# Banded attention scores on the whole array: q's parts stacked by halves, k's parts doubled, and a table of put-off steps

## The chip, the cores and the metric

The kernel runs on one core of one Trainium2 chip. Its engines are TensorE (PE in the profile; PEld are its weight loads), VectorE (DVE), ScalarE (ACT), GpSimd (POOL) and SyncE (SP, which only issues DMAs). The metric is the device time of one execution in microseconds.

## What is computed

Two layers of an encoder over 512 tokens of 1024 channels, all in float32. Each layer projects x to the parts of two token mixers, projects their outputs, merges them by gates, adds and normalises, and then runs a feed-forward part with 4096 hidden channels. The part that matters is mixer A, attention within 128 tokens to either side:

```python
qa = _rope(qa.reshape(bsz, seq, 8, 64), cos, sin)      # 8 heads of 64
ka = _rope(ka.reshape(bsz, seq, 2, 64), cos, sin)      # 2 key heads, 4 queries' heads on each
oa, _ = _banded_attention(qa, ka, va, 128, a_sink)
...
# _banded_attention, for each block j of 128 queries
s = jnp.einsum('nqkgd,nskd->nkgqs', qj * scale, kj)    # kj: three blocks of keys
s = jnp.where(mask, s, -jnp.inf)
m = jnp.maximum(jnp.max(s, axis=-1), sink_b)
e = jnp.exp(s - m[..., None])
denom = jnp.sum(e, axis=-1) + jnp.exp(sink_b - m)
o = jnp.einsum('nkgqs,nskd->nqkgd', e, vj) / denom
```

Mixer B does the same over three groups of heads with dilated windows, without the sink.

## The kernel before

Precision comes from splitting: every operand of a product is kept as a high part in fp32r and a low part, the rest. `split` makes them (ACT copies into the high part, DVE subtracts), and a product is three matmuls: high by high, low by high, high by low (`mm3`, or `PASSES` for scores). Projections stream x (all 512 tokens) through 128x128 tiles of weights, 24 matmuls of 512 columns for an output tile of 128 channels. Weights come in fixed order through SP (`fetch`) and are split by `split`, or by `split_later`, which lets ACT write both parts and a DMA on POOL's queue add the source to the low one.

`attention_block` runs the mixers of a layer. Its start projects k, v and the first two q tiles of mixer A. A tile of q holds two heads, i on rows 0 to 63 and i+4 on rows 64 to 127, and k's tile holds the two key heads on the same halves of rows. `rope` rotates such a tile: DVE shuffles and multiplies, POOL multiplies, DVE adds (`t1`), and `split` gives the pair qh, ql. `pair_scores` (L435) then forms the scores of both heads from halves: a matmul of 64 rows for each head and pass, six of them for a step, of which the two heads' run as a pair.

What PE does when is written out by hand in this block. `unit_a(i)` is a generator of the work for q tile i: four score steps (blocks j, with 256, 384, 384, 256 keys; tiles sa), then transposes of the exponentials (pta) and their products with v (oa), then a scaling. `unit_b` and `mix_b` do that for mixer B. `filler` yields the projections one k-tile (three matmuls) at a time, in the order of `FLOW`: q tiles 2 and 3 of A, then q, k, v of B's groups (qb, kb, vb), gates g(0,t) and the output projections of A (y, tiles ya). The loop at the end of the block takes the first generator whose next step is ready by a forecast (`Forecast`, with assumed durations and `HOP` between engines), else one step of filler; a third count, `held["qk"] - held["free_qk"]`, limits how many q and k tiles are alive (5), and a filler that needs one stands still until a unit has ended its scores. The forecast decides only the order on PE. The other engines' order is set by a scheduler from the program; DVE and ACT serve the masks (`masked`, L432, DVE, reads a score bank), exponentials (L428, ACT) and splits in the order that comes out. There are two PSUM banks for scores, two for transposes, one for oa and three for projections. The name sa_1_2 stands for unit a1, block 2.

Of the kernel before, what the change touches and what calls it, by code (L numbers as in the profile page):

```python
# [10 lines left out]
F32 = mybir.dt.float32  # L11
F32R = mybir.dt.float32r
# [27 lines left out]
ACTIVE = 2  # L40

# [160 lines left out]
def build(nc, tc, plan, down, xT, xN, pT, wst, vec, rows, sink, cst, out):  # L202
# [3 lines left out]
    with ctx:  # L206
# [142 lines left out]
        def attention_block(l, av, rp, vt, OA, OB, begun):  # L349
# [21 lines left out]
            def rope(ps, dil, name):  # L371
# [6 lines left out]
                hi = av.tile([P, S], F32R, tag="qh", name="qh" + name, bufs=5)  # L378
                lo = av.tile([P, S], F32R, tag="ql", name="ql" + name, bufs=5)
# [60 lines left out]

            def weighted(o, vv, blk, r, pT, cols, first, last):
                both = vv[:, blk, r].rearrange("p h d -> p (h d)")
                nc.tensor.matmul(o, both, pT[0][:, cols], start=first, stop=False, skip_group_check=True)
                nc.tensor.matmul(o[:64], both[:, :64], pT[1][:, cols], start=False, stop=last, skip_group_check=True)
# [27 lines left out]
            def unit_a(i):  # L472
                q, k = held["qa", i], held["ka"]
# [245 lines left out]
            held = {"P": 0, "qk": 3, "free_qk": 0, "vv": 0}  # L719
# [6 lines left out]
            held["ka"] = rope(kps, False, f"ka{l}")  # L726
# [3 lines left out]
            held["qa", 0] = rope(q0, False, f"qa{l}_0")  # L730
            fc.take("mm")
            held["qa", 1] = rope(q1, False, f"qa{l}_1")
# [19 lines left out]
            def filler():  # L752
                def project(key, sigma_order):
# [3 lines left out]
                    held[key] = rope(ps, sigma_order, "_".join(str(v) for v in (l, *key)))  # L757

                for kind, *idx in FLOW:
                    if kind == "qa":  # L760
                        yield from project(("qa", *idx), False)
                    elif kind == "b":
# [5 lines left out]
                        side.append([v_unit(("vb", *idx), v, t, nm_), None])  # L768
# [20 lines left out]
            def slots(n, *keys):  # L789
                def ok():  # L790
                    if held["P"] + n > 4 or any(k not in held or fc.t < held[k][2] for k in keys):
# [5 lines left out]
            ga, waiting, live = [], {}, {}  # L797
# [10 lines left out]
            with tc.manual_schedule(engines={PE}):  # L808
                side.append([v_unit("va", va, t_va, f"va{l}"), None])
                fill, fill_ok, idle = filler(), None, 0  # L810
                while waiting or live or side or fill:
                    if waiting and len(live) < ACTIVE:
                        key = next(iter(waiting))
                        ok, make = waiting[key]
                        if ok():
                            del waiting[key]
                            live[key] = [make(), None]
                    moved = False
                    for key, g in [(None, g) for g in side] + list(live.items()):
                        if g[1] is None or g[1]():  # L820
                            try:
                                g[1] = next(g[0])
                            except StopIteration:
# [235 lines left out]
        for l in range(DEPTH):  # L1059
# [33 lines left out]
            for u in range(4):  # L1093
                gs = [gate(l, 1, t, vt, rp) for t in (2 * u, 2 * u + 1)]
# [271 lines left out]
```

## Time and profile before

| | us |
|---|---|
| runs | 1536.09, 1539.66, 1539.62 |
| median | 1539.62 |
| the profiled execution | 1536.4 |
| its span | 1534.6 |
| PE busy in it | 1512.5 (99%) |
| DVE, ACT, POOL busy | 1017.7, 763.7, 246.4 |
| attention stage, layer 0 and layer 1 | 245.70, 247.90 |

The profile is one execution, taken by the hardware profiler; its span is a little shorter than its time. PE's busy time is modelled, and matmuls overlap each other, so how long PE takes for something is read from the starts of matmuls. The attention stage here is the stretch from the transposes of va (29.2 us in layer 0) to the first gate of the second branch (274.9 us).

### The profile page before, as it was taken

The page shows a single profiled execution, that of the slowest core. Times are in us where ns is not written, and L with a number is a line of the kernel's source. Part 1 is how long each engine was busy: PE and PEld are TensorE (multiplying, and loading weights), DVE is VectorE, ACT ScalarE, POOL GpSimd, SP SyncE. Part 2 cuts the span into 40 slices and gives each one's busy share as a digit, 9 for nine tenths or more (in the row PEclk, how much of TensorE's full clock was granted, in tenths as well). Part 3 has the DMA queues.
Part 4 walks back from the last instruction along what each step waited for, and adds up shares of the span by engine and source line. Part 5 has one row for each costly group of instructions (what it writes and reads, how often), then busy time and mean ns, then how long its engine had stood idle before and what let it go on. Part 6 is the DMA issues. An engine that isn't in the chain of part 4 may idle for free.

```text
span 1534.6 us, 19685 instructions
## 1 busy us (share of the span) xinstructions
PE 1512.5 (99%) x7438; PEld 1243.0 (81%) x7438; DVE 1017.7 (66%) x1751; ACT 763.7 (50%) x1244; POOL 246.4 (16%) x213
## 2 busy tenths in 40 slices
PE   9999999999999999999999999999999999999996
PEld 7778888888888888888887888878888888888885
DVE  5666553558568777686876665534585776767868
ACT  5777764344344443444557776633442444444442
POOL 1212220110011120202012112111100201111022
PEclk9999999999999999999999999999999999999998
DMA  7544665345612414141355445574455233231403
GB/s 234 124 112 111 149 151 166 123 137 152 205 55 87 133 54 153 42 161 59 100 168 137 114 112 138 138 209 134 149 149 183 69 109 111 82 124 56 151 1 96
DMA packets 53951, 189.47 MB, mean 123 GB/s; under 512 B 6496, under 2 KB 6880, under 8 KB 53856
## 3 DMA queue, kind: packets, MB, share of 16 engines
q1 hardware_dynamic: 43200, 151.74, 30.0%
q0 software_dynamic: 9936, 36.18, 12.5%
q8 instruction: 58, 0.95, 0.3%
q10 hardware_dynamic: 720, 0.30, 0.1%
q14 instruction: 37, 0.30, 0.1%
HBM read 155.16 MB, written 4.19 MB: 104 GB/s over the span
## 4 chain that ended last, share of the span: by engine, by line
PE 88%; DVE 5%; DMA 3%; ACT 2%; issue 1%; POOL 0%; SPq 0%; POOLq 0%; DVEq 0%; ACTq 0%
PE dn L1018 16%; PE ps_up L281 8%; PE ps_up L280 8%; PE ps_up L282 8%; PE pg L288 2%; PE wo L288 2%; PE wo L287 2%; PE wo L286 2%; PE pg L286 2%; PE pg L287 2%; PE sa L439 1%; PE pta L417 1%; DMA raw<-wst 1%; PE sb L439 1%; PE ps_start L281 1%
## 5 line engine op out<-in xcount | busy, mean ns | idle before, releaser
L228 ACT CAST whi<-wst 128x1024 fp32r<-128x1024 f32 (+2 forms) x120 | 121.2, 1010 | 257.8 <-PE ps_up L281 115.5
L229 DVE TENSOR_TENSOR wlo<-wst,whi 128x1024 fp32r<-128x1024 f32 (+2 forms) x120 | 145.5, 1216 | 128.2 <-ACT whi L228 127.4
L280 PE MATMUL ps_up<-xhi,whi 128*128 128x512 f32 x512 | 199.2, 389 | 0.0
L281 PE MATMUL ps_up<-xlo,whi 128*128 128x512 f32 x512 | 199.2, 389 | 0.0
L282 PE MATMUL ps_up<-xhi,wlo 128*128 128x512 f32 x512 | 199.2, 389 | 0.0
L991 POOL TENSOR_TENSOR hr<-r 128x512 f32<-128x512 f32 x64 | 102.2, 1597 | 552.2 <-ACT r L983 531.7
L280 PEld LDWEIGHTS ps_up<-xhi,whi 128*128 128x128 f32 x512 | 96.1, 188 | 20.0
L282 PEld LDWEIGHTS ps_up<-xhi,wlo 128*128 128x128 f32 x512 | 96.1, 188 | 19.9
L281 PEld LDWEIGHTS ps_up<-xlo,whi 128*128 128x128 f32 x512 | 96.1, 188 | 19.9
L228 ACT CAST whi<-raw 128x1024 fp32r<-128x1024 f32 x56 | 58.0, 1053 | 97.0 <-PE ps_up L281 57.7
L228 ACT CAST dhi<-raw 128x1024 fp32r<-128x1024 f32 x56 | 58.7, 1052 | 82.2 <-PE dn L1018 60.1
L1037 DVE TENSOR_TENSOR y<-y,dn 128x512 f32<-128x512 f32 x96 | 65.0, 681 | 38.7 <-PE dn L1018 38.7
L235 POOL DMA_DIRECT2D wlo<-wst x54 | 47.4, 877 | 244.8 <-ACT wlo L234 157.6
L971 DVE TENSOR_TENSOR raw<-raw,raw 128x1024 f32<-128x1024 f32 x64 | 86.3, 1348 | 0.2
L233 ACT CAST whi<-wst 128x1024 fp32r<-128x1024 f32 x54 | 56.7, 1051 | 42.5 <-PE ps_start L281 6.9
L229 DVE TENSOR_TENSOR wlo<-raw,whi 128x1024 fp32r<-128x1024 f32 x56 | 68.1, 1219 | 14.1 <-ACT whi L228 14.1
L229 DVE TENSOR_TENSOR dlo<-raw,dhi 128x1024 fp32r<-128x1024 f32 x56 | 69.2, 1238 | 5.8 <-ACT dhi L228 5.8
L234 ACT ACTIVATE wlo<-whi 128x1024 fp32r<-128x1024 f32 x54 | 57.3, 1061 | 0.9
L288 PE MATMUL pg<-bhi,xlo 128*128 128x512 f32 x128 | 49.9, 390 | 1.2 <-DVE xlo L915 1.2
L1018 PE MATMUL dn<-whi,smh 128*128 128x512 f32 x128 | 50.1, 394 | 0.7 <-DVE y L1037 0.7
L1018 PE MATMUL dn<-wlo,smh 128*128 128x512 f32 x128 | 50.6, 395 | 0.1
L1018 PE MATMUL dn<-whi,sml 128*128 128x512 f32 x128 | 49.9, 390 | 0.0
(846 smaller groups left out, 4014.0 us busy)
## 6 DMA issues: line engine op xcount, KB each, us to landing
wst<-wst SPq DMA_DIRECT2D x187, 512.0 KB, 3.5
raw<-wst SPq DMA_DIRECT2D x64, 512.0 KB, 4.2
wlo<-wst POOLq DMA_DIRECT2D x54, 512.0 KB, 4.6
y<-rows POOLq DMA_DIRECT2D x14, 512.0 KB, 7.2
row<-rows SPq DMA_DIRECT2D x7, 512.0 KB, 8.8
wst<-wst SPq DMA_DIRECT2D x9, 256.0 KB, 2.7
xs<-xT SPq DMA_DIRECT2D x8, 256.0 KB, 6.0
y<-xN SPq DMA_DIRECT2D x4, 512.0 KB, 5.7
```

What stands on the lines that cost most here:

```text
L228: nc.scalar.copy(hi, src)
L229: nc.vector.tensor_tensor(lo, src, hi.bitcast(F32), ALU.subtract)
L280: nc.tensor.matmul(ps, w[0][:, s], x[0], start=start, stop=False, skip_group_check=part)
L281: nc.tensor.matmul(ps, w[0][:, s], x[1], start=False, stop=False, skip_group_check=part)
L282: nc.tensor.matmul(ps, w[1][:, s], x[0], start=False, stop=stop, skip_group_check=part)
L286: nc.tensor.matmul(ps, x[0], w[0][:, c], start=start, stop=False)
L287: nc.tensor.matmul(ps, x[0], w[1][:, c], start=False, stop=False)
L288: nc.tensor.matmul(ps, x[1], w[0][:, c], start=False, stop=stop)
L971: nc.vector.tensor_tensor(to, to, other, ALU.add)
L991: nc.gpsimd.tensor_tensor(h.rearrange("p s t -> p (s t)"), r, r, ALU.mult)
L1018: nc.tensor.matmul(ps[s], a[:, k, tok], w[b][:, cols], start=first and not (k or m), stop=k == 3 and m == 2, skip_group_check=True)
L1037: return nc.vector.tensor_tensor(to, to, ps, ALU.subtract if n in (2, 4, 5) else ALU.add)
```

## The change

For mixer A's scores, `rope` gets a word `whole`. For a q tile it makes two tiles, one for each head r: the head's high part on its own half of rows (ACT), its low part on the other half (DVE). For k it makes two pairs: the key head's high part on its own half, and the same copied to the other half by a DMA inside SBUF on POOL's queue, and so the low part. `whole_scores` then multiplies over 128 rows: q's stacked parts by the doubled high part of k, and by its doubled low part, so all four products of the parts are in two matmuls for each head. Mixer B's scores still go through `pair_scores`. The tags qh and ql get 6 buffers for 5, and the limit of live tiles goes from 5 to 6, where k counts two. The forecast's cost of a step goes from 6 to 4 passes. A table `LEAVE` names 26 steps of the units (unit, number of the step) which, once ready by the forecast, are put off by so many us; during that time other ready work goes first. The gates' tag is parted in two (8 in the old pool, 3 in another).

```diff
+LEAVE = {
+    ("a", 0, 1): 0.6, ("a", 0, 14): 0.6, ("a", 1, 4): 0.3, ("a", 1, 16): 4.5, ("a", 2, 18): 1.0,
...
+                if whole:
...
+                    both = pair() if whole == "q" else [pair(0), pair(1)]
+                    for r, x in enumerate(both):
+                        own, other = (slice(r * 64, r * 64 + 64), slice(64 - r * 64, P - r * 64))
+                        hi = x if whole == "q" else x[0]
+                        nc.scalar.copy(hi[own], t1[own])
+                        u = fc.on("act", 0.48, t) + HOP
+                        if whole == "q":
+                            nc.vector.tensor_tensor(x[other], t1[own], x[own].bitcast(F32), ALU.subtract)
+                        else:
+                            nc.gpsimd.dma_start(hi[other], hi[own])
+                            nc.vector.tensor_tensor(x[1][own], t1[own], hi[own].bitcast(F32), ALU.subtract)
+                            nc.gpsimd.dma_start(x[1][other], x[1][own])
+                        u = fc.on("dve", 0.6, u) + HOP
+                    return both, u + (0 if whole == "q" else 2.5)
...
+            def whole_scores(ss, q, k, qs, ks, col):
+                for r in range(2):
+                    for n in range(2):
+                        nc.tensor.matmul(ss[r][:, col], q[r][:, qs], k[r][n][:, ks], start=n == 0, stop=n == 1)
...
-                    pair_scores(ss, q, k, slice(j * P, (j + 1) * P), slice(k0, k1), slice(0, w))
-                    fc.pe(6 * w / 2400)
+                    whole_scores(ss, q, k, slice(j * P, (j + 1) * P), slice(k0, k1), slice(0, w))
+                    fc.pe(4 * w / 2400)
...
-                held["free_qk"] += 1 + (i == 3)
+                held["free_qk"] += 1 + 2 * (i == 3)
...
-                    yield lambda: held["qk"] - held["free_qk"] < 5
+                    yield lambda: held["qk"] - held["free_qk"] < 6
...
+            def left(g):
+                more = LEAVE.get((*g[2], g[3]), 0)
+                if not more or not g[1]():
+                    return not more and g[1]()
+                since.setdefault((*g[2], g[3]), fc.t)
+                return fc.t >= since[(*g[2], g[3])] + more
...
-                        if g[1] is None or g[1]():
+                        if g[1] is None or left(g):
...
-            g = rp.tile([P, S], F32, tag="gate", name=f"gate{l}_{b}_{t}", bufs=11)
+            g = rp.tile([P, S], F32, tag=f"gate{b}", name=f"gate{l}_{b}_{t}", bufs=3 if b else 8)
...
-                gs = [gate(l, 1, t, vt, rp) for t in (2 * u, 2 * u + 1)]
+                gs = [gate(l, 1, t, vt, np1) for t in (2 * u, 2 * u + 1)]
```

Three places show how the order on the engines changes. The first is PE in unit a1 of layer 0, from the last score matmul of block 2 on. Before, it reads so, and five more such triples of the projection of qb follow ahead of sa_1_3:

```order
L439 MATMUL sa_1_2_1_642<-qhka_301,qlqa_1_324 128x384
L443 MATMUL oa_0_0_604<-ptha_0_2_613,vvva_338 128x384
L444 MATMUL oa_0_0_604<-ptla_0_2_614,vvva_338 64x384
L417 MATMUL pta_0_4_658<-ident,pa_0_1_397 128x128 x3
L280 MATMUL ps_('qb', 0, 0)_637<-xhi,whi_443 128x512
L281 MATMUL ps_('qb', 0, 0)_637<-xlo,whi_443 128x512
L282 MATMUL ps_('qb', 0, 0)_637<-xhi,wlo_444 128x512
```

Now block 3 follows at once:

```order
L478 MATMUL sa_1_2_1_677<-ql1ka_304,qlqa_1_334 128x384
L482 MATMUL oa_0_0_652<-ptha_0_2_661,vvva_350 128x384
L483 MATMUL oa_0_0_652<-ptla_0_2_662,vvva_350 64x384
L451 MATMUL pta_0_4_691<-ident,pa_0_1_417 128x128 x3
L478 MATMUL sa_1_3_0_699<-qh0ka_301,qhqa_1_333 128x256
L478 MATMUL sa_1_3_0_699<-ql0ka_302,qhqa_1_333 128x256
L478 MATMUL sa_1_3_1_700<-qh1ka_303,qlqa_1_334 128x256
L478 MATMUL sa_1_3_1_700<-ql1ka_304,qlqa_1_334 128x256
L289 MATMUL ps_('kb', 0, 0)_724<-xhi,whi_510 128x512
```

The 18 projection matmuls that stood between the two score steps now stand earlier (those of qb) or behind (kb); only two matmuls of oa and three transposes are left between them.

On DVE at the same place, before, the masks of both heads of block 2 (pa from sa) stand together (an ISA row with one name reads the maximum):

```order
L229 TENSOR_TENSOR ptla_0_2_614<-pta_0_2_609,ptha_0_2_613 128x384
L432 ISA pa_1_0_424,mxa_1_426<-sa_1_2_0_641,ct_157 128x384
L432 ISA mxa_1_426 128x1
L432 ISA pa_1_1_425,mxa_1_426<-sa_1_2_1_642,ct_157 128x384
L432 ISA mxa_1_426 128x1
L229 TENSOR_TENSOR ptla_0_3_625<-pta_0_3_619,ptha_0_3_624 128x512
L493 SCALAR_TENSOR_TENSOR nma_1_427<-mxa_1_426,nsk_160 128x2
L449 TENSOR_TENSOR fa_0_542<-oa_0_0_604,fa_0_542 64x512
```

And now:

```order
L238 TENSOR_TENSOR ptla_0_2_662<-pta_0_2_657,ptha_0_2_661 128x384
L466 ISA pa_1_0_445,mxa_1_447<-sa_1_2_0_676,ct_157 128x384
L466 ISA mxa_1_447 128x1
L388 TENSOR_TENSOR t_qb_0_643<-t_qb_0_643,sw_qb_0_642 128x512
L466 ISA pa_1_1_446,mxa_1_447<-sa_1_2_1_677,ct_157 128x384
L466 ISA mxa_1_447 128x1
L238 TENSOR_TENSOR ptla_0_3_673<-pta_0_3_667,ptha_0_3_672 128x512
L466 ISA pa_1_0_445,mxa_1_447<-sa_1_3_0_699,ct_157 128x256
L466 ISA mxa_1_447 128x1
L488 TENSOR_TENSOR fa_0_570<-oa_0_0_652,fa_0_570 64x512
```

An addition for the rotation of qb (t_qb) has come between the two masks, and the mask of block 3's first head stands ahead of the addition of fa, which frees the bank of oa.

The second place is POOL in the start of layer 0. Before, POOL multiplies for k, q0, q1 and q tile 2, and then issues a weight's DMA (wlo):

```order
L376 TENSOR_TENSOR swka_295<-swka_295,ct_157 128x512
L376 TENSOR_TENSOR swqa_0_307<-swqa_0_307,ct_157 128x512
L376 TENSOR_TENSOR swqa_1_317<-swqa_1_317,ct_157 128x512
L376 TENSOR_TENSOR sw_qa_372<-sw_qa_372,ct_157 128x512
L235 DMA wlo_385<-wst_382 128x1024
```

And now:

```order
L387 TENSOR_TENSOR swka_295<-swka_295,ct_157 128x512
L387 TENSOR_TENSOR swqa_0_315<-swqa_0_315,ct_157 128x512
L408 DMA qh0ka_301<-qh0ka_301 64x512
L408 DMA qh1ka_303<-qh1ka_303 64x512
L387 TENSOR_TENSOR swqa_1_327<-swqa_1_327,ct_157 128x512
L410 DMA ql0ka_302<-ql0ka_302 64x512
L410 DMA ql1ka_304<-ql1ka_304 64x512
L244 DMA wlo_399<-wst_396 128x1024
L387 TENSOR_TENSOR sw_qa_384<-sw_qa_384,ct_157 128x512
```

The four copies of k's parts stand around q1's multiplication, and the weight's DMA has moved ahead of q tile 2's.

The third place is ACT at the end of the attention stage of layer 1, where ph is the split of the embedding's input pf, loaded from HBM, and the gates g(0,6) and g(0,7) free a projection's bank. Before:

```order
L228 CAST whi_9296<-wst_9294 128x1024
L847 ACTIVATE gate_0_6_9292<-ps_('g', 0, 6)_9267,vhalf_6779 128x512
L228 CAST ph_9808<-pf_9810 128x1024
L228 CAST whi_9329<-wst_9327 128x1024
L847 ACTIVATE gate_0_7_9325<-ps_('g', 0, 7)_9300,vhalf_6779 128x512
L228 CAST whi_9363<-wst_9361 128x1024
```

And now:

```order
L237 CAST whi_9264<-wst_9262 128x1024
L894 ACTIVATE gate_0_6_9260<-ps_('g', 0, 6)_9225,vhalf_6763 128x512
L237 CAST whi_9297<-wst_9295 128x1024
L894 ACTIVATE gate_0_7_9293<-ps_('g', 0, 7)_9268,vhalf_6763 128x512
L237 CAST ph_9776<-pf_9778 128x1024
L237 CAST whi_9331<-wst_9329 128x1024
L237 CAST whi_9385<-wst_9383 128x512
```

ph has moved from ahead of gate (0,7) to behind it; the weight casts (whi) keep their places against the gates.

## Rows read from the trace of the kernel before

**Rows 1.** The page of the profile, busy time of an engine (us, share of the span, instructions) and the chain of work that ended last, by engine.

```profile
PE 1512.5 (99%) x7438; PEld 1243.0 (81%) x7438; DVE 1017.7 (66%) x1751; ACT 763.7 (50%) x1244; POOL 246.4 (16%) x213
...
PE 88%; DVE 5%; DMA 3%; ACT 2%; issue 1%; POOL 0%; SPq 0%; POOLq 0%; DVEq 0%; ACTq 0%
```

**Rows 2.** Busy time by stretch; the columns are start:end, length, busy us (and instructions) of PE, of its weight loads, DVE, ACT, POOL, then the granted PE clock, the share of DMA time and GB/s. The stretch runs in layer 0 from the transposes of va to the first gate of the second branch.

```profile
29.20:274.90 245.70, 245.26 (x1429) 199.78 (x1428) 145.98 (x401) 163.31 (x343) 46.18 (x52) 1.00 0.55 139
```

**Rows 3.** PE in order of time around a score step of unit a0 that lies inside the projection of q's tile 3 (start us, busy us, line, operation, out<-in, rows*columns of the array, moving operand; x2 is a pair, one for each head).

```profile
44.01 0.39 PE L281 MATMUL ps_('qa', 3)_448<-xlo,whi 128*128 128x512 f32 x1
44.23 0.39 PE L282 MATMUL ps_('qa', 3)_448<-xhi,wlo 128*128 128x512 f32 x1
44.55 0.45 PE L439 MATMUL sa<-qhka,qhqa 64*128 64x384 f32 x2
44.83 0.34 PE L439 MATMUL sa<-qlka,qhqa 64*128 64x384 f32 x2
45.01 0.34 PE L439 MATMUL sa<-qhka,qlqa 64*128 64x384 f32 x2
45.28 0.50 PE L280 MATMUL ps_('qa', 3)_448<-xhi,whi 128*128 128x512 f32 x1
45.61 0.40 PE L281 MATMUL ps_('qa', 3)_448<-xlo,whi 128*128 128x512 f32 x1
```

**Rows 4.** PE in order of time, columns as before: a projection, matmuls of oa with the whole array, and later a score step of unit a2 with 256 keys.

```profile
69.44 0.39 PE L282 MATMUL ps_('kb', 0, 0)_739<-xhi,wlo 128*128 128x512 f32 x1
69.67 0.33 PE L443 MATMUL oa<-ptha,vvva 128*128 128x384 f32 x1
69.84 0.34 PE L444 MATMUL oa<-ptla,vvva 128*64 128x384 f32 x1
70.01 0.60 PE L462 MATMUL rsa<-ident,widea 128*128 128x128 f32 x4
...
71.20 0.28 PE L439 MATMUL sa<-qlka,qh_qa 64*128 64x256 f32 x2
71.32 0.27 PE L439 MATMUL sa<-qhka,ql_qa 64*128 64x256 f32 x2
```

**Rows 5.** All engines in order of time at the first score step of layer 0; PEld are the loads of a matmul's stationary operand; the bracket is the idle time before, and what ended it.

```profile
36.59 0.21 PEld L439 LDWEIGHTS sa<-qhka,qhqa 64*128 64x128 f32 x2 [0.35 <-issue]
...
37.22 0.19 PEld L439 LDWEIGHTS sa<-qhka,qlqa 64*128 64x128 f32 x2 [0.31 <-DVE qlqa L229]
...
37.53 0.19 PEld L280 LDWEIGHTS ps_('g', 0, 0)_389<-xhi,whi 128*128 128x128 f32 x1
```

**Rows 6.** PE in order of time in the start of layer 1, where the first projections go over 256 columns.

```profile
767.92 0.28 PE L281 MATMUL ps_start<-xlo,whi 128*128 128x256 f32 x1
768.04 0.28 PE L282 MATMUL ps_start<-xhi,wlo 128*128 128x256 f32 x1
```

**Rows 7.** PE in order of time at the transposes of va and the projection behind them.

```profile
29.24 0.60 PE L407 MATMUL vtva<-ident,vTva 128*128 128x128 f32 x4
29.60 0.47 PE L280 MATMUL ps_('qa', 2)_347<-xhi,whi 128*128 128x512 f32 x1
29.91 0.39 PE L281 MATMUL ps_('qa', 2)_347<-xlo,whi 128*128 128x512 f32 x1
30.13 0.39 PE L282 MATMUL ps_('qa', 2)_347<-xhi,wlo 128*128 128x512 f32 x1
```

**Rows 8.** Groups of instructions in the stretch of rows 2, kept apart by shape (busy us in all and mean ns of one, then idle time before them): first DVE, then ACT.

```profile
L432 DVE CUSTOM_DVE_ANT_0 pa<-sa,ct 128x384 f32<-128x384 f32 x16 | 8.3, 553 | 8.7 <-PE sa L439 8.7
...
L449 DVE TENSOR_TENSOR fa<-oa,fa 64x512 f32<-64x512 f32 x8 | 5.5, 686 | 0.6 <-ACT fa L448 0.5
...
L377 DVE TENSOR_TENSOR t_qb<-t_qb,sw_qb 128x512 f32<-128x512 f32 x6 | 4.1, 677 | 0.9 <-POOL sw_qb L376 0.9
...
L234 ACT ACTIVATE wlo<-whi 128x1024 fp32r<-128x1024 f32 x25 | 26.5, 1061 | 0.4
L233 ACT CAST whi<-wst 128x1024 fp32r<-128x1024 f32 x25 | 26.3, 1051 | 17.0 <-PE ps_('g', 0, 5)_2564 L281 3.0 <-PE ps_('vb', 1, 1)_2195 L281 2.2 <-PE ps_('kb', 1, 2)_2355 L281 2.0
```

**Rows 9.** DVE in order of time in the start of layer 0: q0's rotated tile is added up.

```profile
33.73 1.50 DVE L377 TENSOR_TENSOR t1qa<-t1qa,swqa 128x512 f32<-128x512 f32 x1
```

**Rows 10.** The page of the profile, a group of POOL's DMA issues (busy, mean ns of one), and DMA issues by kind (count, KB each, median us from issue to landing).

```profile
L235 POOL DMA_DIRECT2D wlo<-wst x54 | 47.4, 877 | 244.8 <-ACT wlo L234 157.6
...
wlo<-wst POOLq DMA_DIRECT2D x54, 512.0 KB, 4.6
...
wst<-wst SPq DMA_DIRECT2D x9, 256.0 KB, 2.7
```

**Rows 11.** ACT, PE and SP in order of time at the end of the attention stage, of layer 1 (ACT, PE, SP) and of layer 0 (ACT).

```profile
1031.81 1.05 ACT L228 CAST ph<-pf 128x1024 fp32r<-128x1024 f32 x1 [8.75 <-DMA pf<-pT]
...
1033.71 0.68 ACT L847 ACTIVATE gate<-ps_('g', 0, 7)_9300,vhalf 128x512 f32<-128x512 f32 x1
...
1034.44 0.50 PE L280 MATMUL ya<-oah,whi 128*128 128x512 f32 x1 [1.95 <-ACT gate L847]
...
1023.11 0.47 SPq L1112 DMA_DIRECT2D pf<-pT  x1
...
266.71 1.05 ACT L228 CAST ph<-pf 128x1024 fp32r<-128x1024 f32 x1 [6.59 <-DMA pf<-pT]
```

More of the change, by code (lines that the diff above doesn't have):

```diff
@@ L40 @@
 ACTIVE = 2
+LEAVE = {
[6 rows of a table added]
+}
 QB0, KB0, VB0, GL0 = 768, 1536, 2304, 3072
@@ L369, in forecast_split, with rope @@
                 return h, fc.on("dve", 0.07 + n / 960, h + HOP)
-            def rope(ps, dil, name):
+            def rope(ps, dil, name, whole=""):
                 sw = av.tile([P, S], F32, tag="sw", name="sw" + name, bufs=2)
@@ L377, in rope, with pair @@
                 nc.vector.tensor_tensor(t1, t1, sw, ALU.add)
-                hi = av.tile([P, S], F32R, tag="qh", name="qh" + name, bufs=5)
-                lo = av.tile([P, S], F32R, tag="ql", name="ql" + name, bufs=5)
+                def pair(n=""):
+                    return [av.tile([P, S], F32R, tag="q" + e, name=f"q{e}{n}{name}", bufs=6) for e in "hl"]
+                if whole:
+                    a = fc.on("dve", 0.6, fc.t + HOP)
+                    b = fc.on("dve", 0.6, a)
+                    c = fc.on("pool", 1.23, a + HOP)
+                    fc.give("mm", b + HOP)
+                    t = fc.on("dve", 0.6, max(b, c) + HOP) + HOP
+                    both = pair() if whole == "q" else [pair(0), pair(1)]
[12 more added lines that the diff above has]
+                    return both, u + (0 if whole == "q" else 2.5)
+                hi, lo = pair()
                 if dil:
@@ L472, in unit_a @@
             def unit_a(i):
-                q, k = held["qa", i], held["ka"]
+                q, k = held["qa", i][0], held["ka"][0]
                 nm_ = f"a{l}_{i}"
@@ L718, in attention_block @@
             fc = Forecast()
-            held = {"P": 0, "qk": 3, "free_qk": 0, "vv": 0}
+            held = {"P": 0, "qk": 4, "free_qk": 0, "vv": 0}
             if begun:
@@ L725, in attention_block @@
             fc.take("mm")
-            held["ka"] = rope(kps, False, f"ka{l}")
+            held["ka"] = rope(kps, False, f"ka{l}", "k")
             va, t_va = values(vps, "natural", f"va{l}")
@@ L729, in attention_block @@
             fc.take("s", 3.5)
-            held["qa", 0] = rope(q0, False, f"qa{l}_0")
+            held["qa", 0] = rope(q0, False, f"qa{l}_0", "q")
             fc.take("mm")
-            held["qa", 1] = rope(q1, False, f"qa{l}_1")
+            held["qa", 1] = rope(q1, False, f"qa{l}_1", "q")
             side = []
@@ L752, in filler, with project @@
             def filler():
-                def project(key, sigma_order):
-                    yield lambda: held["qk"] - held["free_qk"] < 5
+                def project(key, sigma_order, whole=""):
+                    yield lambda: held["qk"] - held["free_qk"] < 6
                     held["qk"] += 1
                     ps = yield from steps((l, key), X)
-                    held[key] = rope(ps, sigma_order, "_".join(str(v) for v in (l, *key)))
+                    held[key] = rope(ps, sigma_order, "_".join(str(v) for v in (l, *key)), whole)
                 for kind, *idx in FLOW:
                     if kind == "qa":
-                        yield from project(("qa", *idx), False)
+                        yield from project(("qa", *idx), False, "q")
                     elif kind == "b":
@@ L767, in filler @@
                         v, t = values(ps, "sigma" if idx[1] else "edge", nm_)
-                        side.append([v_unit(("vb", *idx), v, t, nm_), None])
+                        side.append([v_unit(("vb", *idx), v, t, nm_), None, ("vb", *idx), 0])
                     elif kind == "g":
@@ L790, in ok @@
                 def ok():
-                    if held["P"] + n > 4 or any(k not in held or fc.t < held[k][2] for k in keys):
+                    if held["P"] + n > 4 or any(k not in held or fc.t < held[k][-1] for k in keys):
                         return False
@@ L795, in slots @@
                 return ok
-            ga, waiting, live = [], {}, {}
+            def left(g):
[4 more added lines that the diff above has]
+                return fc.t >= since[(*g[2], g[3])] + more
+            ga, waiting, live, since = [], {}, {}, {}
             for i in range(4):
@@ L808, in attention_block @@
             with tc.manual_schedule(engines={PE}):
-                side.append([v_unit("va", va, t_va, f"va{l}"), None])
+                side.append([v_unit("va", va, t_va, f"va{l}"), None, ("va",), 0])
                 fill, fill_ok, idle = filler(), None, 0
@@ L816, in attention_block @@
                             del waiting[key]
-                            live[key] = [make(), None]
+                            live[key] = [make(), None, key, 0]
                     moved = False
                     for key, g in [(None, g) for g in side] + list(live.items()):
-                        if g[1] is None or g[1]():
+                        if g[1] is None or left(g):
                             try:
                                 g[1] = next(g[0])
+                                g[3] += 1
                             except StopIteration:
```

5 rows, old and new, of the table LEAVE are left out of this document.

## The prediction

> **What bounds the kernel now.** I read the busy table and the chain of work first. PE is busy 1512.5 of 1534.6 us, 99%, and 88% of the chain that ended last is PE work [rows 1]: time is lost or won only where PE does less or waits less. Then I read the stretches. Layer 0's attention stage, from the transposes of va to the first gate of the second branch, is 245.70 us with PE busy 245.26 of them at a granted clock of 1.00, the upper of its two levels (2.4 GHz) [rows 2]. So PE hardly waits there, and its time must come from how its instructions follow each other. That is the third view, PE in order of time. The profile's PE "busy" is modelled; what counts is the distance from one start to the next. A 512-column matmul follows another after 0.22 to 0.23 us, a pair of 64-row matmuls of 384 columns after 0.18 (44.83 to 45.01) [rows 3], a pair of 256 after 0.12 (71.20 to 71.32) [rows 4]. But a score step inside projections costs more than its columns. From the last projection matmul before it (44.23) to the second one behind it (45.61) are 1.38 us [rows 3]. In there are two 512-column matmuls and three pairs of 384: 2 x 0.227 + 3 x 0.173 = 0.97 us. The other **0.40 us** is paid at the way in (0.32 instead of 0.23, then 0.28 instead of 0.17) and at the way out (0.27 instead of 0.17, then 0.33). The weight loads show the same place: the 64-row load starts with its matmul, not ahead of it, and so does the first 128-row load behind (37.53, the start of its matmul) [rows 5].
>
> **The change, part by part.**
>
> *Columns.* Before, a step is three pairs; a pair takes the distance of one matmul. After, it is four 128-row matmuls, two heads by two parts of k. What a 128-row matmul of 256 columns costs is in the trace: 0.12 us, one behind the other [rows 6], the same as a pair of halves; 384 columns take 0.17 (69.67 to 69.84) [rows 4]. So each step gains one distance: per unit 2 x 0.120 + 2 x 0.173 = 0.586, four units 2.34 us, **+2.3 us a layer**.
>
> *Switches.* Sixteen steps a layer pay 0.40 now: 6.4 us. Do 128-row scores pay something of the kind? The nearest rows are 128-row oa matmuls behind a projection: 69.44, 69.67, 69.84, 70.01 [rows 4], distances 0.23, 0.17, 0.17; nothing is paid. Behind transposes something is: the matmul after four of them is followed 0.31 later instead of 0.23 [rows 7], 0.09 more. In the new PE order transposes meet 128-row matmuls seven times more a layer, since those beside scores were inside the 0.40 before: 7 x 0.09 = 0.6. So **-6.4 + 0.6 = -5.8 us a layer**. Group B's scores stay on halves. Columns and switches together are -3.5 a layer, -7.0 in all. Bounds: -12.8 + 4.7 = -8.1 if transposes cost nothing more, and the slower rival below.
>
> The Trainium skill's page "TensorEngine Tiling (Array Packing)", section "Theoretical Speedup", speaks against this edit: a contraction of 64 rows or less is worth splitting the array for, up to twice as fast. By that rule alone the sum would hold the +2.3 a layer without the switches, and the kernel would lose. The trace agrees with it on the columns, 0.12 for a pair against 0.12 for one whole matmul.
>
> *Start of a layer.* Of k, ACT now copies and DVE subtracts two halves instead of one whole, and four copies of 128 KB go through POOL's queue; of each q there are two copies and two subtractions of 64 x 512. A half is not cheaper on DVE: 64x512 takes 686 ns and 128x512 677 [rows 8]. Before, the first score pairs waited 0.31 us for qlqa [rows 5]. After, PE has 15 matmuls of g(0,0) ahead of them instead of 6 and gets there 9 x 0.227 = 2.0 us later, at about 38.6. DVE: t1qa's addition ends near 35.2 [rows 9]; two subtractions for k and two for q at 0.6 each end near 37.6, under that cover. The copies: k's low halves are ready near 35.8 and 36.4, and an issue holds POOL 0.88 us [rows 10], so the last is issued near 36.7. What such a copy takes isn't in the trace. The nearest rows are 2.7 us for 256 KB on SP's queue and 4.6 for 512 KB through POOL [rows 10]. With 2.7 it lands at 39.4, for the fourth score matmul at 38.6 + 3 x 0.12 = 39.0: a wait of 0.4. With 4.6 it is 2.3. I take 2.7, since the copy is the smaller transfer: **+0.1 a layer** net of the 0.31; below it, -0.3. POOL's other work queued behind the four issues, q1's multiplication and the next weights' DMA, comes some 2 us later; its readers on PE are behind 9 more projection matmuls.
>
> *Crowded place.* The planner lets six q and k tiles live, k's two pairs count twice, and when they are gone nothing fills PE until unit a1's scores are done. Before, 18 projection matmuls and two others stand between the scores of sa_1_2 and sa_1_3. After, only two oa matmuls and three transposes do, 2 x 0.173 + 3 x 0.109 + a distance, some 0.85 us. There are two banks for scores; the second head's bank is free only when DVE has gone through the mask of sa_1_2's first head, an addition of t_qb that now stands between, and the mask of the second: 0.55 + 0.6 + 0.55 = 1.7 us [rows 8]. DVE gets the first head some 0.15 after the last score matmul of sa_1_2 starts, and on PE the second head of sa_1_3 comes two matmuls later: it waits 0.15 + 1.7 - 0.85 - 2 x 0.12 = 0.75. Then fa's addition holds the bank of oa_0_1, 0.15 by the same counting, and pta_1_0 waits for the last exponentials, 0.45. That is **+1.35 a layer**, +2.7 in all. Bounds: zero, if DVE has run ahead; and if ACT takes a weight's two steps ahead of an exponential, 1.05 + 1.06 = 2.1 more [rows 8], 3.5. I take the middle counting because the order on DVE fixes that addition between the two masks.
>
> *End of layer 1.* Before, ACT's ph waited 8.75 us for pf from HBM with gate (0,7) behind it; the matmul of ya that needs a PSUM bank of that gate waited 1.95 us [rows 11]. In layer 0 ph waited 6.59 too, but PE did not stop there. After, ph stands behind gate (0,7). What is late next is what stands behind ph, a weight cast for g(1,1), which PE reads only after the 48 matmuls of the last two ya and the 24 of g(1,0), 16 us; pf's 8.7 us from issue [rows 11] end inside them. So **-1.95**, once; bounds -1.95 and 0.
>
> *The rest* is priced at zero: the other put-off steps only change which ready PE work goes first; gates in two tags keep as many buffers; POOL's and SP's moved DMAs belong to weights that are read tens of matmuls later. If that cover were gone, a weight's delay by one 0.88 us issue is the price.
>
> *Sum* against the profiled run's own 1536.4 us: -7.0 + 0.2 + 2.7 - 1.95 = -6.05, so 1530.3. The median of the runs is 3.2 us above the profiled run; I take the difference over: 1539.6 - 6.05 = **1533.6 us**, -0.39%.
>
> **The rivals.**
>
> *The crowded place costs its upper bound*, 3.5 us a layer. For it: nothing is left there to fill PE with, and ACT, DVE and PE wait for each other in turn. Against: ACT is busy only half of the time. -7.0 + 0.2 + 7.0 - 1.95 = -1.75: 1537.9.
>
> *k's copies land late*, 2.3 us after PE wants them. For it: POOL's queue showed 4.6 [rows 10]; against: for four times the bytes. The sum gets 2 x 1.9 worse than with 0.4: -2.25, 1537.4.
>
> *The stall of layer 1 does not go*, or moves to the next cast: -4.1, 1535.5. For it: pf was the last DMA in both layers.
>
> *The waits are hidden*: no crowded place, -8.75, 1530.9.
>
> *Slower*: the 0.40 us belongs to any short group of score matmuls with fresh weights, not to the split rows. Then the steps keep it and only the columns count: +4.7 + 0.2 + 2.7 - 1.95 = +5.65, **1545.3**. It decides below some (5.65 + 1.25) / 32 = 0.21 us saved a step; the 1.25 are the transposes. Against it stand the oa rows, short 128-row groups with fresh weights at 0.17 [rows 4], and the weight load that starts only with its matmul at the 64-row steps [rows 5].
>
> The skill's same page, section "Key Properties", says that changing the tiling mode drains TensorE. By that the 0.40 goes with the split rows, which speaks against the slower rival; but it would also charge the oa matmuls that change between 128*128 and 128*64, and those rows show 0.17, the bare distance [rows 4]. So I don't lean on it.
>
> **How the numbers follow.** Chances: forecast 0.45; crowded place 0.20; late copies 0.10; stall stays 0.08; waits hidden 0.09; slower rival 0.08. A measurement of this kernel tells about 0.3%, 4.6 us, from no change. Forecast and hidden waits are faster by more: 0.54. Crowded, late and staying stall are within: 0.38. Slower 0.08. The range: downwards the hidden waits with 2 us for the median's place among runs that lie 3.6 us apart, 1529; upwards the crowded place with the same 2 us, 1540. It leaves out the slower rival and little else.
>
> **What would show it.** Score matmuls in 128*128 form, with starts 0.12 and 0.17 apart and 0.23 to the projections around them; the stretch from the transposes of va to the first gate of the second branch shorter by some 2 us in layer 0 and 4 in layer 1; a wait of about 0.4 us at the first score group on a DMA of k; waits of about 0.75, 0.15 and 0.45 us near the fourth score step of a1, on DVE and ACT; no wait for gate (0,7) at the last ya. I am wrong if 128-row scores pay at their edges, if the waits at a1 sum to 3 us or more, or if new waits show up where the fillers give out later.

## The result, and the profile after

| | before | after |
|---|---|---|
| runs (us) | 1536.09, 1539.66, 1539.62, 1540.16 | 1530.95, 1530.64, 1529.32, 1530.17 |
| median | 1539.64 | 1530.41 |
| the profiled execution, its span | 1536.4, 1534.6 | 1530.95, 1529.2 |
| attention stage, layer 0 and 1 | 245.7, 247.9 | 243.8, 244.1 |

The ratio is 0.9945, with a 95% interval of 0.9931 to 0.9958: the change makes the kernel 0.55% faster. From profile to profile the gain is 5.45 us, where the sum said 6.05; from median to median it is 9.2. Where the difference comes from is the subject of the second and third part of the experiments.

The page's busy line and chain, and the attention stages by stretch, answer [rows 1, 2]:

```profile
PE 1506.9 (99%) x7374; PEld 1249.8 (82%) x7374; DVE 1030.7 (67%) x1761; ACT 768.2 (50%) x1254; POOL 250.9 (16%) x221
...
PE 87%; DVE 6%; ACT 2%; DMA 2%; issue 2%; POOL 0%; SPq 0%; POOLq 0%; ACTq 0%; DVEq 0%
```

```profile
29.60:273.40 243.80, 242.29 (x1397) 203.10 (x1396) 152.20 (x406) 165.63 (x348) 48.35 (x56) 1.00 0.56 143
791.80:1035.90 244.10, 242.41 (x1397) 203.10 (x1396) 152.57 (x406) 165.70 (x347) 52.01 (x60) 1.00 0.57 143
```

The chain is still PE's. DVE has 6 us more work in layer 0's stage and ACT 2.3, as the halves cost; PE has 3 us less. PE in order of time at a score step between projection matmuls, the counterpart of [rows 3]:

```profile
46.54 0.39 PE L290 MATMUL ps_('qa', 3)_460<-xlo,whi 128*128 128x512 f32 x1
46.77 0.39 PE L291 MATMUL ps_('qa', 3)_460<-xhi,wlo 128*128 128x512 f32 x1
46.99 0.33 PE L478 MATMUL sa<-qh0ka,qhqa 128*128 128x384 f32 x1
47.17 0.34 PE L478 MATMUL sa<-ql0ka,qhqa 128*128 128x384 f32 x1
47.34 0.34 PE L478 MATMUL sa<-qh1ka,qlqa 128*128 128x384 f32 x1
47.52 0.34 PE L478 MATMUL sa<-ql1ka,qlqa 128*128 128x384 f32 x1
47.69 0.39 PE L289 MATMUL ps_('qa', 3)_460<-xhi,whi 128*128 128x512 f32 x1
47.92 0.40 PE L290 MATMUL ps_('qa', 3)_460<-xlo,whi 128*128 128x512 f32 x1
```

From 46.77 to 47.92 are 1.15 us, and 2 x 0.227 + 4 x 0.173 is 1.15: the edges cost nothing. Before, the same stretch took 1.38.

The waits of PE in layer 0's stage, in one list (what waited, for what; us in total, times, longest), are these:

```profile
PE sa L478 <- DVE mxa L466: 0.5, 1, 0.5
PE rs L501 <- ACT wide L495: 0.4, 1, 0.4
PE sa L478 <- DMA ql0ka<-ql0ka: 0.2, 1, 0.2
PE ptb L451 <- ACT pb L462: 0.2, 1, 0.2
```

The first and the third were forecast, at 0.75 and 0.4; the other two, in mixer B, were not. Around each the starts of matmuls lose some tenths more than the list shows, since PE picks up again with a late weight load.

### The profile page after: what moved, and what is told of

Read it like the earlier page. It is cut to its first block, busy times and chain, and to the rows that moved or that the text cites. A ratio compares the mean times of both kernels' runs of the same rounds, so it can differ in the third digit from the quotient of the medians.

```text
span 1529.2 us, 19607 instructions
## 1 busy us (share of the span) xinstructions
PE 1506.9 (99%) x7374; PEld 1249.8 (82%) x7374; DVE 1030.7 (67%) x1761; ACT 768.2 (50%) x1254; POOL 250.9 (16%) x221
## 4 chain that ended last, share of the span: by engine, by line
PE 87%; DVE 6%; ACT 2%; DMA 2%; issue 2%; POOL 0%; SPq 0%; POOLq 0%; ACTq 0%; DVEq 0%
PE dn L1065 17%; PE ps_up L291 8%; PE ps_up L289 8%; PE ps_up L290 8%; PE wo L297 2%; PE pg L297 2%; PE pg L295 2%; PE pg L296 2%; PE wo L296 2%; PE wo L295 2%; PE pta L451 1%; PE sb L473 1%; PE sa L478 1%; PE ya L289 1%; PE ya L291 1%
## 5 line engine op out<-in xcount | busy, mean ns | idle before, releaser
L1065 PE MATMUL dn<-dhi,smh 128*128 128x512 f32 x128 | 49.9, 390 | 0.0
```

Of the source, the lines that this page charges most:

```text
L1065: nc.tensor.matmul(ps[s], a[:, k, tok], w[b][:, cols], start=first and not (k or m), stop=k == 3 and m == 2, skip_group_check=True)
```

## The experiments

Medians, with the ratio to the kernel before measured beside each:

| kernel | median us | ratio, 95% interval |
|---|---|---|
| before_again | 1538.44 | 0.9990, 0.9981 to 0.9999 |
| halves | 1538.91 | 0.9994, 0.9985 to 1.0002 |
| no_table | 1544.07 | 1.0028, 1.0019 to 1.0038 |
| gates_only | 1540.70 | 1.0004, 0.9994 to 1.0014 |
| ph_later | 1535.59 | 0.9971, 0.9960 to 0.9983 |
| ct_later | 1530.26 | 0.9938, 0.9925 to 0.9950 |
| k_direct | 1532.65 | 0.9954, 0.9941 to 0.9966 |
| qb_pool | 1530.04 | 0.9936, 0.9922 to 0.9949 |
| before_table | 1540.56 | 1.0003, 0.9993 to 1.0012 |
| after_again | 1530.46 | 0.9943, 0.9927 to 0.9958 |
| both | 1528.80 | 0.9932, 0.9918 to 0.9947 |
| before_third | 1541.24, one run | |

before_again is the kernel before, unchanged, and its interval still leaves out 1 by a little: differences of 0.1% decide nothing here, and two kernels that were measured at different times are better compared by their ratios. The experiments ask whether the 0.40 us belongs to split rows or to any short group of scores, whether the table carries the gain, and where single waits come from.

### Do the switches belong to the split rows? (halves)

```diff
 def whole_scores(ss, q, k, qs, ks, col):
-    for r in range(2):
-        for n in range(2):
-            nc.tensor.matmul(ss[r][:, col], q[r][:, qs], k[r][n][:, ks], start=n == 0, stop=n == 1)
+    for n in range(3):
+        for r in range(2):
+            rows = slice(64 * r, 64 * r + 64)
+            nc.tensor.matmul(ss[r][:, col], q[r ^ (n == 2)][rows, qs], k[r][n % 2][rows, ks], start=n == 0, stop=n == 2)
```

> The changed kernel with the order, table, tiles and copies as they are, only group A's scores again as six 64-row matmuls a step, in pairs (the third product takes the low part of the other head's q, since the own one lies on the other half; the work is the same). Theory (the 0.40 us a step belongs to split rows): columns -2.3, switches +5.8 a layer, 7 us slower than the changed kernel, some 1537.5 us; starts 0.32 and 0.28 us apart at the steps' edges again. Rival (the 0.40 us belongs to any short group of scores): 4.7 us faster than the changed kernel, some 1525.7 us.

Measured: 8.5 us slower than the changed kernel by the medians (1538.91 against 1530.41), 7.5 by the ratios (0.9994 against 0.9945). The attention stages are 3.6 us longer in layer 0 and 3.1 in layer 1, 6.6 in all against the 7 expected. The rest lies behind the attention, most of it in PE's wait for xlo, 1.4 us here and none in the profile of the changed kernel; that wait differs from profile to profile (below). The step of the rows above, in this kernel:

```profile
46.22 0.39 PE L291 MATMUL ps_('qa', 3)_462<-xhi,wlo 128*128 128x512 f32 x1
46.54 0.44 PE L479 MATMUL sa<-qh0ka,qhqa 64*128 64x384 f32 x1
...
46.82 0.33 PE L479 MATMUL sa<-ql1ka,qlqa 64*128 64x384 f32 x1
...
47.00 0.34 PE L479 MATMUL sa<-qh1ka,qhqa 64*128 64x384 f32 x1
...
47.26 0.50 PE L289 MATMUL ps_('qa', 3)_462<-xhi,whi 128*128 128x512 f32 x1
```

The distances are 0.32, 0.28, 0.18 and 0.26 again, with the same tiles, copies and table. The switches belong to the split rows, and the rival that would have made the change slower is out. The Trainium skill's page "TensorEngine Tiling (Array Packing)", section "Key Properties", says that a change of tiling mode drains the engine; these edges agree with it, at 0.40 us a visit, but the oa matmuls that alternate between 128*128 and 128*64 still show the bare distance [rows 4].

### What is the table worth? (no_table, before_table)

no_table:

```diff
-LEAVE = {
-    ("a", 0, 1): 0.6, ("a", 0, 14): 0.6, ("a", 1, 4): 0.3, ("a", 1, 16): 4.5, ("a", 2, 18): 1.0,
...
-}
+LEAVE = {}
```

> The changed kernel with an empty table of put-off steps. The steps of a1 stand as they do with the table, so the wait of 0.64 us there stays. Theory: PE's switches are 0.3 us a layer less, and the waits in mixer B's units grow by 0 to 2 us a layer; 1530 to 1534 us. Rival: the table carries the gain by hiding waits of 3 us and more a layer; 1536 us or more.

Measured: 13.6 us slower than the changed kernel by the medians, 12.8 by the ratios, and slower than the kernel before. The rival is right that there is no gain without the table. Layer 0's stage is 248.3 us (243.8 with the table), layer 1's 253.3 (244.1). PE's longest waits over the whole execution:

```profile
PE oa L476 <- DVE ptla L231: 4.0, 6, 0.9
PE ya L282 <- ACT gate L887: 2.9, 1, 2.9
PE dn L1058 <- DVE y L1077: 2.1, 5, 0.8
PE ps_start L284 <- DMA wlo<-wst: 1.5, 1, 1.5
PE oa L475 <- DVE fa L481: 1.1, 4, 0.3
PE ob L475 <- DVE ogb L481: 1.0, 2, 0.5
```

The oa rows are the table's work: PE reaches a product with v before DVE has the low part of the transposed exponentials (ptla), and stands; with the table a put-off step lets a projection go first, and these rows are gone from the list of the changed kernel. The ya row is another effect: without the table ph stands ahead of gate (0,7) again, and behind that wait eight matmuls go 0.43 us apart. So of the 9.2 us by which layer 1's stage is longer some 4.5 are ph's place, which comes with the table and has nothing to do with scores.

before_table, the other half alone: the table and `left` in the kernel before.

```diff
+LEAVE = {
+    ("a", 0, 1): 0.6, ("a", 0, 14): 0.6, ("a", 1, 4): 0.3, ("a", 1, 16): 4.5, ("a", 2, 18): 1.0,
...
-                        if g[1] is None or g[1]():
+                        if g[1] is None or left(g):
```

> The kernel before with the table of put-off steps and the code that reads it, nothing else: scores on halves, old gates, old limit. In its program ph stands behind gate (0,7), as in the changed kernel. Theory: the table by itself brings what ph behind that gate brings, 4.5 us, and 0.2 us of switches a layer; waits elsewhere change by less than 1 us a layer: 1534 to 1537 us. Rival: the table fits only the new scores, and costs waits here: 1540 us or more.

Measured: no difference from before, 1.0003. The rival is nearer. Layer 0's stage grows from 245.7 to 249.9 us by new waits of 3.0 us and, behind the last two of them, half a dozen matmuls at the lower clock level. Layer 1's, at 248.3, has the same waits without that drop, and no wait for gate (0,7), which costs the kernel before more than this in its slower executions (next part); so the two cancel. The waits in layer 0's stage, and the stretch behind the sb rows in layer 0 and in layer 1 (columns as in [rows 2]):

```profile
PE oa L452 <- DVE fa L458: 1.9, 2, 1.1
PE sb L448 <- DVE ql_kb L238: 0.7, 1, 0.7
PE sb L448 <- ACT qh_kb L237: 0.4, 1, 0.4
```

```profile
228.00:232.00 4.00, 4.00 (x14) 3.24 (x13) 0.65 (x8) 3.49 (x17) 0.00 (x0) 0.70 0.75 261
995.00:999.00 4.00, 4.00 (x20) 3.30 (x19) 0.56 (x6) 3.19 (x16) 0.00 (x0) 1.00 0.76 263
```

So neither half helps by itself: whole scores without the table are 0.28% slower than before, the table without them is even, both together are 0.55% faster. The table's numbers fit one order of work. The sixth buffer and the limit of 6 live tiles were not tried by themselves.

### Why is the kernel before mostly 3 to 4 us above its profiled execution? (before_again, before_third, ph_later)

> The kernel before, unchanged, as a measure of the spread. Theory: ratio 1.000 within 0.2%; executions near 1536 and near 1540 us both turn up, and a profile near 1540 would show a few waits of PE of one to three us that the profile at 1536.4 lacks, on DMAs or on DVE. Rival: the spread lies evenly over all PE work; then no single wait of that size differs.

> The kernel before once more, for a profile. Theory: an execution near 1540 us has the wait for gate (0,7) at some 4 us and the granted clock at 0.50 behind it for a dozen matmuls, 0.43 us apart instead of 0.23; one near 1536 us has 1.95 us and no drop. Rival: the wait is 1.95 us in both, and another place differs.

Measured: before_again ran from 1534.95 to 1541.23, and its profile, of 1535.41, has the wait for gate (0,7) at 1.9 us, as [rows 11]. before_third was caught at 1541.24. Of it, PE and ACT in order of time at the end of layer 1's stage, and the stretches there (columns as in [rows 2]):

```profile
1031.83 0.39 PE L282 MATMUL ya<-oah,wlo 128*128 128x512 f32 x1
1036.19 0.80 PE L280 MATMUL ya<-oah,whi 128*128 128x512 f32 x1 [3.98 <-ACT gate L847]
1036.79 0.63 PE L281 MATMUL ya<-oal,whi 128*128 128x512 f32 x1
1037.21 0.63 PE L282 MATMUL ya<-oah,wlo 128*128 128x512 f32 x1
...
1033.56 1.04 ACT L228 CAST ph<-pf 128x1024 fp32r<-128x1024 f32 x1 [11.07 <-DMA pf<-pT]
...
1035.46 0.68 ACT L847 ACTIVATE gate<-ps_('g', 0, 7)_9300,vhalf 128x512 f32<-128x512 f32 x1
```

```profile
1034.00:1038.00 4.00, 1.81 (x4) 1.49 (x5) 3.36 (x4) 3.19 (x4) 0.00 (x0) 0.57 1.07 316
1038.00:1042.00 4.00, 4.00 (x12) 3.09 (x11) 1.68 (x3) 0.00 (x0) 0.00 (x0) 0.58 1.05 261
1042.00:1046.00 4.00, 4.00 (x19) 3.30 (x18) 1.63 (x3) 0.62 (x1) 0.00 (x0) 1.00 0.48 188
```

pf lands 2.3 us later than in the first profile (ph waited 11.07, not 8.75), the wait is 3.98, and then the granted clock falls to its lower level: matmuls go 0.43 us apart instead of 0.23 for a dozen. Layer 1's stage is 252.5 us instead of 247.8. These 4.7 us are nearly all that lies between the two executions (4.84): 2.0 are the longer wait, and from the matmul that ends it to the end of the stage 2.4 more go by at the lower clock (8.0 us instead of 5.6). A second kernel with ph ahead of the gate, gates_only of the next part, was caught at 1541.54 and shows the same, a dozen matmuls at 0.43 behind this row:

```profile
1037.60 0.80 PE L280 MATMUL ya<-oah,whi 128*128 128x512 f32 x1 [3.86 <-ACT gate L847]
```

Why pf lands later in one execution than in another stays open.

The theory written for before_third holds to the number, with one correction: the stretch shows 0.57 and 0.58 where it said 0.50, since it holds matmuls at either level.

ph_later takes the cause away in the kernel before:

```diff
 nc.sync.dma_start(pf, pT[l])
-split(ph, pl, pf)
+with tc.issue_after(mark["seven"].ins):    # gate (0,7) on ACT
+    split(ph, pl, pf)
```

> The kernel before, with ACT's split of pf held behind gate (0,7) and nothing else. Theory: in most executions of the kernel before pf lands later than in the profiled one, and ph holds gate (0,7) and PE for 4 to 6 us, not 1.95; so this kernel is 4 to 5 us faster than before in the median, some 1535 us, and its runs lie within 2 us of each other, as those of the changed kernel do. Rival: the wait is always near 1.95 and the spread has another source; 2 us faster in the median, the runs still 6 us apart.

Measured: 4.5 us faster than before in the median, 0.9971, as the theory said; its profile has no wait for that gate. The second half of the theory fails: its runs still lie 4.5 us apart (1532.75 to 1537.30). So this wait is the larger part of the 3 to 4 us, but the spread has other sources too, and those stay open. It also parts the gain of the change: beside ph_later, a kernel before that is free of this wait, the changed kernel is some 5 us faster (1530.41 against 1535.59, measured at different times). The other half of the 9.2 us is ph's place, which one ordering hint gives as well, without any new scores.

### Single waits (gates_only, ct_later, qb_pool, k_direct, both)

gates_only puts the gates' two tags into the kernel before:

```diff
-g = rp.tile([P, S], F32, tag="gate", name=f"gate{l}_{b}_{t}", bufs=11)
+g = rp.tile([P, S], F32, tag=f"gate{b}", name=f"gate{l}_{b}_{t}", bufs=3 if b else 8)
...
-gs = [gate(l, 1, t, vt, rp) for t in (2 * u, 2 * u + 1)]
+gs = [gate(l, 1, t, vt, np1) for t in (2 * u, 2 * u + 1)]
```

> The kernel before with the gates' tag parted in two and nothing else; PE's order stays, the load of ct moves ahead of two stores on SP. Theory: the 1.5 us wait at the start of layer 1, for wlo behind ct's 960 KB, shows here too, the attention stages stay at 245.7 and 247.8 us; 0 to 1.5 us slower than before. Rival: that wait comes of the new attention order, and is not here; equal to before within 0.5 us.

ct_later puts the load of ct back behind the stores of kept in the changed kernel:

```diff
 if begun:
-    load_constants()
+    with tc.issue_after(mark["kept"].ins):    # the last store of kept on SP
+        load_constants()
```

> The changed kernel with the load of ct for layer 1 held behind the last store of kept, its place before the change. Theory: the 1.5 us that PE waits for wlo at the start of layer 1 is wlo's DMA sharing the engines with ct's 960 KB; it goes, and wlo lands some 6.5 us after its issue instead of 10.6: 1.5 us faster than the changed kernel, some 1529 us. Rival: wlo is late by the stores of kept or by its own issue: no difference.

Measured: gates_only, 1.0004, not told from before; in its profile PE waits 1.6 us for wlo at the start of layer 1, with nothing of the attention changed. So the wait comes of the gates' memory. The changed kernel has it too; PE, and the DMAs issued around it (KB each, us to landing):

```profile
767.57 0.39 PE L291 MATMUL ps_start<-xhi,wlo 128*128 128x256 f32 x1 [1.50 <-DMA wlo<-wst]
```

```profile
kept<-y SPq DMA_DIRECT2D x2, 512.0 KB, 6.4
ct<-cst SPq DMA_DIRECT2D x1, 960.0 KB, 6.8
wlo<-wst POOLq DMA_DIRECT2D x1, 512.0 KB, 10.6
```

and in ct_later:

```profile
wlo<-wst POOLq DMA_DIRECT2D x1, 512.0 KB, 6.4
```

ct_later has no such wait. Its median, 1530.26, is not told apart from the changed kernel's 1530.46 (after_again): the mechanism is shown, its worth in the median is not. In two other profiles with ct in the early place (k_direct, qb_pool) ct's issue itself took 1.2 and 1.4 us and wlo landed after 8.7 and 8.5, in time.

qb_pool moves one addition per layer to POOL in the changed kernel:

```diff
-nc.vector.tensor_tensor(t1, t1, sw, ALU.add)
+(nc.gpsimd if name == f"{l}_qb_0_0" else nc.vector).tensor_tensor(t1, t1, sw, ALU.add)
```

> The changed kernel with the addition of t_qb of the first group of mixer B on POOL instead of DVE. Theory: that addition between the two masks of sa_1_2 is what the second head of sa_1_3 waits for, 0.5 to 0.64 us; the wait goes: 0.5 us a layer, 1 us in all, faster than the changed kernel. Rival: the masks alone set that wait: it stays, no difference.

It is the crowded place. DVE and PE there in the changed kernel, in order of time:

```profile
64.67 0.56 DVE L466 CUSTOM_DVE_ANT_0 pa<-sa,ct 128x384 f32<-128x384 f32 x1
...
65.16 0.69 DVE L388 TENSOR_TENSOR t_qb<-t_qb,sw_qb 128x512 f32<-128x512 f32 x1
65.76 0.55 DVE L466 CUSTOM_DVE_ANT_0 pa<-sa,ct 128x384 f32<-128x384 f32 x1
```

```profile
65.61 0.28 PE L478 MATMUL sa<-ql0ka,qhqa 128*128 128x256 f32 x1
66.37 0.38 PE L478 MATMUL sa<-qh1ka,qlqa 128*128 128x256 f32 x1 [0.47 <-DVE mxa L466]
```

The addition stands between the two masks, and PE loses 66.37 - 65.61 - 0.12 = 0.64 us. With it on POOL the stages are 243.3 and 243.6 us, 0.5 us shorter each, and the wait is not in the list of PE's waits: the theory holds for the stages. The median, 1530.04, is by itself not told apart from the changed kernel's.

k_direct writes k's other halves by ACT and DVE:

```diff
-nc.gpsimd.dma_start(hi[other], hi[own])
+nc.scalar.copy(hi[other], t1[own])
 nc.vector.tensor_tensor(x[1][own], t1[own], hi[own].bitcast(F32), ALU.subtract)
-nc.gpsimd.dma_start(x[1][other], x[1][own])
+nc.vector.tensor_tensor(x[1][other], t1[own], hi[own].bitcast(F32), ALU.subtract)
```

> The changed kernel without k's four DMAs: ACT and DVE write the other halves too, two more copies and two more subtractions of 64x512 a layer. Theory: the waits of the first score step on the copies (0.4 us in layer 0, 0.4 in layer 1) go, but DVE's list ahead of it is 1.2 us longer and ends near 38.8, just where PE comes: within 0.5 us a layer of the changed kernel. Rival (the copies' landing sets that wait, DVE has cover): 0.6 us a layer faster. Other rival: DVE is the bound there, 1 us a layer slower.

Measured: layer 0's stage is 3.0 us longer, layer 1's 0.3 shorter, and the median 2.2 longer (1.4 by the ratios): the second rival, in layer 0, and worse than it said. The first score step there on PE, DVE beside it, and the stretch behind it:

```profile
38.72 0.28 PE L478 MATMUL sa<-ql0ka,qhqa 128*128 128x256 f32 x1
40.68 0.36 PE L478 MATMUL sa<-qh1ka,qlqa 128*128 128x256 f32 x1 [1.68 <-DVE t1qa L386]
...
38.47 0.69 DVE L406 TENSOR_TENSOR qlqa<-t1qa,qlqa 64x512 fp32r<-64x512 f32 x1
...
39.84 0.69 DVE L386 TENSOR_TENSOR t1qa<-ps_start,ct 128x512 f32<-128x512 f32 x1
...
42.00:46.00 4.00, 4.00 (x12) 3.13 (x11) 2.52 (x8) 3.17 (x5) 0.00 (x0) 0.59 0.48 111
```

PE waits 1.7 us, and the granted clock is 0.59 in the 4 us from 42.0. The wait isn't for the halves themselves, of which the last is done at 39.16. The row names the multiplication that reads q1's projection out of PSUM and stands behind the added subtractions in DVE's order. That is what the theory, which counted DVE's work up to the halves, left out. The copies by DMA are the better choice here.

both joins ct_later and qb_pool:

> The changed kernel with ct's load behind the stores of kept and the addition of t_qb on POOL. Theory: the two waits (0.5 us a layer, 0 to 1.5 us at the start of layer 1) are on the path and add up: 1 to 2.5 us faster than the changed kernel in this call, some 1528.5 us. Rival: what they free is waited for behind them; within 0.5 us of the changed kernel.

> The changed kernel, unchanged, to compare with in this call. Theory: 0.9940 of the kernel before, 1530.4 us, with runs within 2 us. Rival: its gain was of the day; 0.997 or more.

Measured side by side: after_again 1530.46 us, 0.9943; both 1528.80, 0.9932. The gain of the change repeats, and the two edits add 1.7 us, with stages of 243.3 and 243.5 us and no wait for wlo. It is the fastest kernel of this study.

## Why the prediction was right, point by point

**Columns and switches**, -3.5 us a layer: right, by the distances of the new score step and by halves, which gives 3.6 and 3.1 us back.

**Start of a layer**: the mechanism right, the size too small. The two low halves, issued when the weight loads were nearly through, landed after 2.7 and 2.5 us, against the 2.7 taken from the row; the two high halves, issued beside weight loads, took 5.5 and 5.8, but had the time. The last copy was issued at 37.40, not 36.7, since t1qa's addition on DVE ended at 35.79 instead of 35.2. PE lost 0.4 us at the first low half (0.50 between two starts where 0.12 would do) and 0.2 at the second (0.33), 0.6 against 0.4, and 0.1 more at the matmul behind each. The Trainium skill's page "DMA: Bandwidth & Descriptors", section "Anatomy of one DMA — SWDGE (gpsimd) path", fits 2.0 us and the bytes over 436 KB a us; for 128 KB that is an estimate of 2.3 us, and only the low halves come near it.

**Crowded place**: the right place and mechanism, half the size. The second head waits 0.64, not 0.75; the bank of oa and the exponentials, 0.15 and 0.45, do not show. About as much as was overcounted there turned up in mixer B, at rs and ptb, which the sum had at nothing. By profile the stages came out at -1.9 and -3.8 us, forecast -2.05 and -4.0.

**End of layer 1**: right in the profiled execution, 1.95 us, and mis-sized for the median, and with it the step "I take the difference over". That carried the 3.2 us between the median and the profiled run into the forecast as if they stayed. They were in large part this same wait, longer in the slower executions and followed by the lower clock: some 4.5 us in the median by ph_later, where the term stood at 1.95. In the changed kernel they are gone with it; its profiled run is not below its median. That is why 9.2 us came where 6.05 were forecast. The forecast counted ph's new place as part of the change, but no part of the new scores brings it: it comes with the table.

**The rest, priced at zero**: wrong in both directions. SP's moved load of ct cost 1.5 us in the profile; that the weights were read tens of matmuls later was true of the wrong ones, as this wlo is read by the third matmul of layer 1. A wait of 1.16 us for xlo in layer 1 before is absent after; it lies between 0.6 and 1.3 us in the three profiles of the kernel before and between nothing and 1.4 in all of this study, so I put it down to the execution. That these two nearly cancel, and the profiles come out within 0.6 us of the sum, is luck. The table was priced as order alone. That the sum came out rested on it, since the sum was counted on the order that the table had made: without the table the same scores gain nothing.

**The rivals**: the slower one is ruled out by halves, the late copies by their landing, the stall that stays by the profile after; the crowded place at its upper bound and the hidden waits are both ruled out by the 0.64 us measured there.

## What to carry to other kernels

Read where a kernel's own runs differ before a change is sized: a wait that one profile shows at 2 us may be 4 us and a clock drop in others, and an edit that removes it gains the larger figure. A wait for a transfer should not stand ahead of short work that frees a bank. When a planner's order is retuned together with the work it orders, take both apart: here each half alone gave nothing or a loss, and the order carried a side effect, ph's place, that was half of the gain.

## What the runs showed of the hardware

Three pairs of 64-row matmuls between 128-row ones cost 0.40 us beyond their columns, in the kernel before and in halves; four 128-row matmuls in the same place cost nothing beyond them.

A wait of PE of 3.98 us was followed by a dozen matmuls at the lower clock level, 0.43 us apart, which cost 2.4 us more; behind the 1.95 us of [rows 11] and the 1.50 us for wlo no such drop showed, behind the 1.68 us of k_direct one did. In before_table two waits of 0.42 and 0.73 us, one microsecond apart, were followed by half a dozen such matmuls in layer 0, and the same two (0.40 and 0.74) by none in layer 1. The length of the wait alone does not decide it here, and what does stays open.

A weight's DMA of 512 KB on POOL's queue landed 6.4 us after issue beside two stores of 512 KB (ct_later), and after 10.6 us in the changed kernel, where 960 KB more were queued on SP at the same moment (8.5 and 8.7 us in qb_pool and k_direct, where that issue itself took 1.2 us and more).
